# Two 384-byte tiles change pools and a 128-byte pad is added, so that most SBUF tiles begin at one address modulo 512

## The chip, the cores and the metric

The kernel runs on one core of a Trainium2 chip. The metric is the device time of one execution in microseconds. A core has a matrix engine (PE; its weight loads stand apart as PEld), a vector engine (DVE), a scalar engine (ACT), a general engine (POOL) and a queue engine (SP). All tiles that are named below lie in the on-chip memory SBUF, which has 128 partitions; an address is the byte at which a tile begins in each partition. PE writes its sums to PSUM, which the change does not touch.

## The reference, cut to what matters

One decoder layer on a sequence of 512 tokens of 1024 channels, in float32:

```python
mod = jax.nn.silu(c) @ w_ada[l] + b_ada[l]
sh1, sc1, g1, sh2, sc2, g2 = jnp.split(mod[:, None, :], 6, axis=-1)
h = modulate(rmsnorm(x, norm_mix_g[l]), sh1, sc1)
x = x + g1 * hybrid_mixer(h, ...)
h = modulate(rmsnorm(x, norm_ffn_g[l]), sh2, sc2)
x = x + g2 * swiglu(h, w_ffn_gate[l], w_ffn_up[l], w_ffn_down[l])
```

`hybrid_mixer` projects `h` to queries, keys, values and gates, runs two kinds of attention with 8 heads of 64 channels each, projects both results (`w_proj_a`, `w_proj_b`), mixes them with sigmoid gates and applies `w_out`. `swiglu` is `(silu(h @ w_gate) * (h @ w_up)) @ w_down` with 2816 inner channels. A last RMSNorm follows.

## The kernel before

Every product keeps float32 accuracy with three matmuls: an operand is split into a high part (`_hi`, or index 0) and the rest (`_lo`, or index 1), and PE adds high by high, high by low and low by high. A weight slab is loaded by a DMA into a tile `raw`; ACT copies its high part into a tile `hl`, DVE subtracts to get the low part. The `mm3` helper issues the three matmuls of one 128-channel step.

A matmul has two operands in SBUF. The stationary one, 128 columns, is loaded by PEld ahead of the matmul; the moving one, mostly 512 columns, streams through. They are, stage by stage, in the order of time (microseconds of the profiled execution):

- 0 to 75: first norm, transposes of `x` (tile `xt`), and the first projections; the values of the second attention have `h_hi`, `h_lo` stationary and `wvh` moving.
- 75 to 330: the other projections (stationary `hl`, moving `h_hi` or `h_lo`; outputs `mm`), interleaved with both attentions. Their matmuls have queries, keys, values and probabilities (`qa`, `qb`, `kb`, `ks`, `kw`, `vn`, `vball`, `ph`, `pl`, `E`) on both sides, and 128-column transposes with the constant `ident` moving.
- 343 to 417: eight blocks of the projected attention (`add_y`): stationary `hl`, moving `oah`, `oal`, `obh` (outputs `s`, `acc`), with gate projections (stationary `hl`, moving `h_hi`, `h_lo`, outputs `mm`) between them. 192 matmuls have `oah`, `oal` or `obh` moving.
- 417 to 465: `w_out` (`token_nodes`): stationary slices of `y`, moving `hl` or, for one of the four weight groups in the second half, `hlw`. 192 matmuls.
- 468 to 482: first feed-forward unit: stationary `hlk`, moving halves (256 columns) of `h_hi`, `h_lo`. 96 matmuls.
- 482 to 712: 21 feed-forward units (`ffn_unit`): stationary `hl`, moving `h_hi`, `h_lo`. 1008 matmuls.
- 712 to 835: down projection (`token_nodes`): stationary slices of `ah`, `al`, moving `hl`. 528 matmuls. The final norm follows.

The order on each engine comes from a list scheduler (`Sched`) that runs while the program is built, with its own table of costs; line 200, which the profile names for nearly every instruction, is its recording helper, so groups are told apart by tiles.

SBUF is handed out by tile pools. Pools lie one after the other in the order in which they are opened; a pool that is closed gives its room to those opened later. In order: `const`, `strm` (`raw`, `hl`), `hp` (`h_hi`, `h_lo`), `small`, `vx` (`vball`, `m0`, `x1t`), `att` (queries, keys, `vn`, `oah`, `oal`, `obh`, `hlk`, `hlw`), then `start`, later `ab` and `wk` or `yp` in its place (`ph`, `pl`, `E`, `y`). When `att` is closed, `fp` (`ah`, `al`, `sgt`, `gfb`, `o`) begins where `att` began. Tiles that share a tag take turns in the same buffers. Within a tile, the slices that PE reads begin at multiples of 512 bytes, except the 280-column weight rows (1120 bytes apart) and the 32-column slices of `kc`.

The two tiles that move are `gat` (the sigmoid gates of the first attention, written by ACT, read by DVE) and `sums` (row sums written by ACT, read by DVE). PE reads neither.

Of the kernel before, what the change touches and what calls it, by code (L numbers as in the profile page):

```python
# [6 lines left out]
F32 = mybir.dt.float32  # L7
# [7 lines left out]
NT = 4  # L15
# [273 lines left out]
def block_kernel(tc, x, c, w_ada, b_ada, norm_mix_g, w_in, cmp_pos_k, cmp_w1_k, cmp_w2_k,  # L289
# [19 lines left out]
    const = es.enter_context(tc.tile_pool(name="const", bufs=1))  # L309
    strm = es.enter_context(tc.tile_pool(name="strm", bufs=2))  # L310
    hp = es.enter_context(tc.tile_pool(name="hp", bufs=1))
    small = es.enter_context(tc.tile_pool(name="small", bufs=4))

    ident = const.tile([128, 128], F32, name="ident")
    make_identity(tc.nc, ident)
# [2 lines left out]

    vec = const.tile([128, 96], F32, name="vec")
    csil = const.tile([128, KT], F32, name="csil")  # L320
    VEC = {"gmix": 0, "bada": 8, "gffn": 56, "posk": 64, "posv": 80}

    def split_act(hi, lo, src):
# [64 lines left out]
    def fin_a(dst, sc, g, kk):  # L388
        nc.vector.scalar_tensor_tensor(dst[:, kk], sc[:, kk], 1.0, vec[:, VEC[g] + kk.start:VEC[g] + kk.stop],
                                       op0=OP.add, op1=OP.mult)  # L390

    def cols_of(ps, acc, dst, chunk, k0, n):
        for j in range(n):
            nc.tensor.matmul(ps[:, j:j + 1], acc[:, j * 128:(j + 1) * 128], ones[:, 0:1], start=True, stop=True)
        b = vec[:, VEC["bada"] + chunk * 8 + k0: VEC["bada"] + chunk * 8 + k0 + n]
        nc.vector.tensor_tensor(dst[:, k0:k0 + n], ps[:, 0:n], b, op=OP.add)
# [1 line left out]
    vx = es.enter_context(tc.tile_pool(name="vx", bufs=1))  # L398
    mid = ExitStack()
    att = mid.enter_context(tc.tile_pool(name="att", bufs=1))  # L400
    gat = att.tile([128, NT, 24], F32, name="gat")

    def qtile(name):
        return att.tile([128, S], R, name=name, tag="q2", bufs=10)
# [40 lines left out]

    kc = att.tile([128, 2, 64], R, name="kc")
    vcs = att.tile([64, 2, 2, 64], R, name="vcs")
    sums = att.tile([128, NT, 24], F32, name="sums")

    pss = ExitStack()  # L450
    pool = pss.enter_context(tc.tile_pool(name="psum", bufs=2, space=PS, reuse_waits="tile"))
# [11 lines left out]
    def stage_load(q, keys):  # L463
        for key, ap, n in (("gmix", norm_mix_g[0], 8), ("bada", b_ada[0], 48), ("gffn", norm_ffn_g[0], 8),
                           ("posk", cmp_pos_k[0].rearrange("j d -> (j d)"), 16),
                           ("posv", cmp_pos_v[0].rearrange("j d -> (j d)"), 16)):
            if key in keys:
                q.dma_start(stage[VEC[key]:VEC[key] + n] if VEC[key] < 56 else stage2[VEC[key] - 56:VEC[key] - 56 + n], rows(ap))

# [213 lines left out]
    def compress(which):  # L683
# [5 lines left out]
        def evac(last, fc, hmm):  # L689
# [13 lines left out]
            hi = lo = None  # L703
            pcol = vec[:, VEC[pos]:VEC[pos] + 16]
            for half in range(2):
# [111 lines left out]
    def add_ada(chunk, nh, dst, row, acc_tag, keys=(), rec=None):  # L817
# [19 lines left out]
        def post():  # L837
# [3 lines left out]
            else:  # L841
                o = VEC["bada"] + chunk * 8 + nh * 4
                nc.vector.tensor_tensor(dst[:, nh * 4:nh * 4 + 4], ps[:, 0:4], vec[:, o:o + 4], op=OP.add)
# [425 lines left out]
    def ada1_nodes(ci, n_cs, n_vec):  # L1269
# [37 lines left out]
        def fin():  # L1307
            for j in range(n):
                k = k0 + j
                g, b = VEC["gmix"] + k, VEC["bada"] + k  # L1310
                nc.scalar.activation(shcol[:, k:k + 1], cell["ps"][:, n + j:n + j + 1], AF.Identity, bias=vec[:, b:b + 1])
# [610 lines left out]
```

## Time and profile before

| | us |
|---|---|
| timed runs | 844.59, 842.13, 841.99; median 842.13 |
| span of the profiled execution, first to last instruction | 843.0 |
| PE busy | 810.5 |
| PEld busy | 664.7 |
| DVE busy | 512.9 |
| ACT busy | 390.2 |
| POOL busy | 37.5 |

The profile gives the profiled execution's span; no time outside the span is listed for it. Its 843.0 us lie inside the range of the three timed runs. A matmul's end is modelled in the profile and overlaps the next one's start, so a matmul's "duration" is longer than the distance to the next; distances are best read from the chain, where a piece gives the time of so many matmuls in a row.

### The profile page before, as it was taken

How to read it: one execution, taken by the hardware profiler on the slowest of the kernel's cores; microseconds unless marked ns; L12 is line 12 of the kernel's file. 1: busy time of each engine (PE TensorE's matmuls, PEld its weight loads, DVE VectorE, ACT ScalarE, POOL GpSimd, SP SyncE). 2: the span in 40 equal slices, each digit the busy share in tenths (PEclk: the TensorE clock that was granted, in tenths of full speed). 3: DMA queues.
4: the chain of work that ended last, by engine and by line, in shares of the span. 5: the costliest groups of instructions: out<-in, count | busy, mean ns of one | idle time of the engine just before them, and what ended most of it. 6: DMA issues, size and time to landing. Idle time of an engine off the chain costs nothing.

```text
span 843.0 us, 10574 instructions
## 1 busy us (share of the span) xinstructions
PE 810.5 (96%) x3881; PEld 664.7 (79%) x3881; DVE 512.9 (61%) x961; ACT 390.2 (46%) x737; POOL 37.5 (4%) x76
## 2 busy tenths in 40 slices
PE   5999998999999999999999899999999999999996
PEld 4777786788787887888888878888888888888884
DVE  3879988998789887755786653443333333225225
ACT  5566755566777887333444632232232223223123
POOL 3002203020000000000000000000000000000000
PEclk9999999999999999999999999999999999999998
DMA  9974233365311010773661463443333332232302
GB/s 285 314 205 125 76 82 119 101 156 138 88 51 50 1 51 26 225 222 114 214 219 31 126 195 114 140 128 99 100 101 100 100 95 89 92 100 84 110 7 100
DMA packets 130732, 100.56 MB, mean 119 GB/s; under 512 B 3804, under 2 KB 110404, under 8 KB 130680
## 3 DMA queue, kind: packets, MB, share of 16 engines
q1 hardware_dynamic: 129448, 96.59, 38.7%
q0 software_dynamic: 1136, 3.27, 1.6%
q8 instruction: 30, 0.49, 0.3%
q14 instruction: 22, 0.18, 0.1%
q10 hardware_dynamic: 96, 0.03, 0.0%
HBM read 95.12 MB, written 2.10 MB: 115 GB/s over the span
## 4 chain that ended last, share of the span: by engine, by line
PE 76%; DVE 10%; DMA 5%; ACT 5%; issue 2%; SPq 2%; POOL 1%; DVEq 0%; POOLq 0%; ACTq 0%
PE mm L200 31%; PE s L200 25%; PE acc L200 17%; PE tp L200 4%; DVE Rb L200 2%; SPq L200 2%; DVE hl L200 1%; DVE a L200 1%; DMA raw<-in_w_ada_dram 1%; DVE ada L200 1%; ACT hl L200 1%; DMA xt<-in_x_dram 1%; DMA wv<-in_w_in_dram 1%; DMA raw<-in_w_in_dram 1%; DMA kw<-kw 1%
## 5 line engine op out<-in xcount | busy, mean ns | idle before, releaser
L200 ACT ACTIVATE hl<-raw 128x1024 fp32r<-128x1024 f32 (+2 forms) x118 | 124.3, 1055 | 288.6 <-issue 142.1
L200 PE MATMUL mm<-h_hi,hl 128*128 128x512 f32 x736 | 249.4, 398 | 0.8 <-ACT s L200 0.8
L200 DVE TENSOR_TENSOR hl<-raw,hl 128x1024 fp32r<-128x1024 f32 (+2 forms) x118 | 143.3, 1215 | 151.5 <-ACT hl L200 151.1
L200 PEld LDWEIGHTS mm<-h_hi,hl 128*128 128x128 f32 x736 | 139.0, 189 | 28.9 <-ACT s L200 1.3
L200 PE MATMUL mm<-h_lo,hl 128*128 128x512 f32 x368 | 144.2, 392 | 0.2 <-DVE h_lo L200 0.2
L200 PEld LDWEIGHTS mm<-h_lo,hl 128*128 128x128 f32 x368 | 69.6, 189 | 12.9 <-DVE h_lo L200 0.6
L200 PE MATMUL s<-h_hi,hl 128*128 128x512 f32 x208 | 66.7, 391 | 0.0
L200 PE MATMUL acc<-h_hi,hl 128*128 128x512 f32 x208 | 66.1, 389 | 0.0
L200 PE MATMUL mm<-hl,ah 128*128 128x512 f32 x176 | 55.2, 395 | 0.0
L200 PE MATMUL s<-hl,ah 128*128 128x512 f32 x176 | 55.2, 395 | 0.0
L200 ACT ACTIVATE ph<-tp 128x512 fp32r<-128x512 f32 (+1 forms) x72 | 36.1, 524 | 21.1 <-PE tp L200 16.0
L200 PEld LDWEIGHTS s<-h_hi,hl 128*128 128x128 f32 x208 | 39.0, 188 | 8.3 <-issue 0.2
L200 DVE TENSOR_TENSOR pl<-tp,ph 128x512 fp32r<-128x512 f32 (+1 forms) x72 | 40.9, 597 | 7.6 <-ACT ph L200 7.3
L200 PEld LDWEIGHTS acc<-h_hi,hl 128*128 128x128 f32 x208 | 39.1, 188 | 8.1
L200 PE MATMUL s<-h_lo,hl 128*128 128x512 f32 x104 | 40.5, 389 | 0.0
L200 PE MATMUL acc<-h_lo,hl 128*128 128x512 f32 x104 | 40.5, 389 | 0.0
L200 ACT ACTIVATE E<-T,m 128x256 f32<-128x256 f32 (+3 forms) x64 | 35.4, 554 | 9.3 <-DVE m L200 8.8
L200 PEld LDWEIGHTS s<-hl,ah 128*128 128x128 f32 x176 | 33.2, 188 | 7.7
L200 PEld LDWEIGHTS mm<-hl,ah 128*128 128x128 f32 x176 | 33.1, 188 | 7.7
L200 PE MATMUL mm<-hl,al 128*128 128x512 f32 x88 | 34.7, 395 | 0.0
L200 PE MATMUL s<-hl,al 128*128 128x512 f32 x88 | 34.7, 395 | 0.0
L200 DVE SCALAR_TENSOR_TENSOR adaacc<-raw,csil,adaacc 128x512 f32<-128x512 f32 x42 | 31.0, 746 | 5.8 <-DMA raw<-in_w_ada_dram 5.4
(281 smaller groups left out, 1326.5 us busy)
## 6 DMA issues: line engine op xcount, KB each, us to landing
raw<-in_w_in_dram SPq DMA_DIRECT2D x32, 512.0 KB, 4.7
raw<-in_w_ada_dram SPq DMA_DIRECT2D x32, 512.0 KB, 4.1
raw<-in_w_ffn_gate_dram SPq DMA_DIRECT2D x22, 512.0 KB, 3.9
raw<-in_w_ffn_up_dram SPq DMA_DIRECT2D x22, 512.0 KB, 5.0
raw<-in_w_ffn_down_dram SPq DMA_DIRECT2D x22, 512.0 KB, 3.9
adaraw<-in_w_ada_dram SPq DMA_DIRECT2D x32, 256.0 KB, 5.4
raw<-in_w_out_dram SPq DMA_DIRECT2D x8, 512.0 KB, 4.7
xt<-in_x_dram SPq DMA_DIRECT2D x4, 512.0 KB, 6.5
```

What stands on the lines that cost most here:

```text
L200: return f(*args, **kw)
```

## The change

`gat` and `sums`, 384 bytes per partition each, are taken from the pool `const` and no longer from `att`; an unused tile of 128 bytes is opened first in the pool `small`. So `strm` and `hp` begin 768 bytes later, `vx` and what follows 896 bytes later, and what follows the two tiles in `att` 512 or 128 bytes later than before.

```diff
     small = es.enter_context(tc.tile_pool(name="small", bufs=4))
+    small.tile([128, 32], F32, name="pad", tag="pad", bufs=1)
...
     csil = const.tile([128, KT], F32, name="csil")
+    gat = const.tile([128, NT, 24], F32, name="gat")
+    sums = const.tile([128, NT, 24], F32, name="sums")
...
     att = mid.enter_context(tc.tile_pool(name="att", bufs=1))
-    gat = att.tile([128, NT, 24], F32, name="gat")
...
     vcs = att.tile([64, 2, 2, 64], R, name="vcs")
-    sums = att.tile([128, NT, 24], F32, name="sums")
```

The addresses modulo 512 at which tiles begin in the two built programs:

| tiles | pool | before | after |
|---|---|---|---|
| `raw`, `hl` | strm | 320 | 64 |
| `h_hi`, `h_lo` | hp | 320 | 64 |
| `vball`, `m0`, `x1t` | vx | 192 | 64 |
| `kc`, `vcs` | att | 64 | 64 |
| queries, keys, `vn`, `wvh`, `oah`, `oal`, `obh`, `hlk`, `hlw` | att | 448 | 64 |
| `xt` | start | 448 | 64 |
| `ph`, `pl`, `E`, `a`, `y` | wk, yp | 448 | 64 |
| `ah`, `al`, `sgt`, `gfb`, `o` | fp | 192 | 64 |
| `ident`, `ones` | const | 128 | 128 |
| `csil` | const | 0 | 0 |
| `adaraw` | start | 96 | 224 |

So four kinds of tile that PE reads are not at 64 afterwards: `ident`, `ones`, `csil` and `adaraw`. They serve the transposes and the small conditioning products.

On every engine the two programs have the same instructions in the same order. One wait differs: POOL's DMA that loads `gfb` waits for one more DMA queue.

## Rows read from the trace of the kernel before

**Rows 1.** The page: span, busy time by engine, granted clock in 40 slices

```profile
span 843.0 us, 10574 instructions
...
PE 810.5 (96%) x3881; PEld 664.7 (79%) x3881; DVE 512.9 (61%) x961; ACT 390.2 (46%) x737; POOL 37.5 (4%) x76
...
PEclk9999999999999999999999999999999999999998
```

**Rows 2.** Stretches: length, busy time (instructions) of PE, PEld, DVE, ACT, POOL; clock; DMA

```profile
343.20:416.90 73.70, 73.70 (x323) 59.85 (x323) 47.86 (x62) 27.56 (x37) 0.00 (x0) 1.00 0.64 195
...
482.00:701.00 219.00, 218.85 (x963) 180.26 (x962) 86.19 (x99) 63.99 (x83) 0.00 (x0) 1.00 0.40 115
712.00:834.90 122.90, 122.89 (x529) 99.28 (x527) 42.81 (x62) 29.64 (x41) 0.00 (x0) 1.00 0.24 78
```

**Rows 3.** The chain, last feed-forward units and down projection: start, us, what, matmuls

```profile
592.50 10.88 PE mm L200 x48
...
712.19 2.79 PE mm L200 x12
...
834.91 0.02 issue
```

**Rows 4.** The chain through `add_y` and `w_out`, same columns

```profile
343.19 2.79 PE s L200 x12
...
354.38 5.45 PE mm L200 x24
...
416.90 1.40 PE mm L200 x6
...
439.19 1.64 PE tp L200 x10
440.84 11.26 PE s L200 x48
...
452.97 5.57 PE acc L200 x24
```

**Rows 5.** Matmuls that read `hl`, 600 to 700 us: duration ns min/median/max, starts

```profile
L200 PE MATMUL s<-h_hi,hl x96: 389/389/389, 608.7 to 690.0; 128*128 128x512 f32 x96
```

**Rows 6.** The same view of `hl`, 343.2 to 354.3 us

```profile
L200 PE MATMUL acc<-obh,hl x24: 392/395/398, 345.8 to 354.0; 128*128 128x512 f32 x24
```

**Rows 7.** The same view of `hl`, 354.6 to 359.6 us

```profile
L200 PE MATMUL mm<-h_hi,hl x16: 389/389/393, 354.2 to 359.4; 128*128 128x512 f32 x16
```

**Rows 8.** The same view of `hlw`, 447.0 to 447.5 us

```profile
L200 PE MATMUL s<-hlw,y x3: 389/389/393, 446.8 to 447.3; 128*128 128x512 f32 x3
```

**Rows 9.** The same view of `hl`, 448.4 to 451.2 us

```profile
L200 PE MATMUL s<-hl,y x13: 392/398/398, 448.2 to 451.0; 128*128 128x512 f32 x13
```

**Rows 10.** The same view of `hl`, 720 to 830 us

```profile
L200 PE MATMUL s<-hl,ah x168: 390/393/404, 720.4 to 825.9; 128*128 128x512 f32 x168
```

**Rows 11.** The same view of `hlk`, 474 to 481.4 us; the chain there

```profile
L200 PE MATMUL s<-h_hi,hlk x17: 278/281/285, 473.9 to 481.2; 128*128 128x256 f32 x17
...
478.69 2.86 PE s L200 x24
```

**Rows 12.** The chain, 240 to 330 us: shares by line; one piece

```profile
by line: PE mm L200 37.3%; PE acc L200 23.4%; PE s L200 21.2%; PE tp L200 17.2%; ACT half L200 0.7%; ACT oah L200 0.6%; issue 0.0%
...
244.27 2.08 PE mm L200 x9
```

**Rows 13.** The chain, 75 to 240 us, then 0 to 75 us: shares by line

```profile
by line: PE mm L200 29.6%; DVE Rb L200 10.3%; PE tp L200 6.9%; DVE a L200 6.8%; PE acc L200 6.1%; issue 4.4%; DVE hl L200 4.2%; PE s L200 4.1%; DMA kw<-kw 3.5%; DVE pl L200 3.4%; POOL a L200 3.3%; DVE qa L200 2.5%; ACT hl L200 2.3%; DVE kb 
...
by line: SPq L200 17.0%; DVE ada L200 9.7%; DMA xt<-in_x_dram 8.7%; DMA wv<-in_w_in_dram 8.2%; DMA raw<-in_w_in_dram 7.9%; PE mm L200 7.5%; DMA adaraw<-in_w_ada_dram 7.2%; issue 4.8%; ACT hl L200 4.2%; DVE kb L200 3.7%; PE tp L200 3.5%; ACT
```

**Rows 14.** Instructions that write or read `gfb`: duration ns, starts

```profile
L200 DVE TENSOR_TENSOR x1t<-x1t,gfb x4: 679/682/691, 763.3 to 777.2; 128x512 f32<-128x512 f32 x4
...
L200 POOL DMA_DIRECT2D gfb<-in_norm_final_g_dram x1: 542/542/542, 466.3 to 466.3; - x1
...
DMA to landing us min/median/max: 6.1/6.1/6.1
```

## The prediction

> **What bounds the kernel now.** I read the page first. PE is busy for 810.5 of 843.0 us and the granted clock is at or near full speed in every slice, its level of 2.4 GHz [rows 1]. PE being busy does not yet mean that it sets the end, so I read the stretches and the chain next. Between 343 and 417, 482 and 701, 712 and 834.9 us PE has next to no idle time, DVE is busy for 65%, 39% and 35% of the stretch and ACT for 37%, 29% and 24%, all at a clock of 1.00 [rows 2]. The chain there is matmul after matmul [rows 3, 4]. From 240 to 330 us PE also holds 99.1% of the chain [rows 12]. From 75 to 240 us its lines hold 46.7%, and before 75 us about 11% [rows 13]. So from about 240 us on, time that a matmul saves is time off the end; earlier, less than half of it is.
>
> Then I asked what a matmul costs. The instruction is the same in both halves of the feed-forward network, 128 by 128 stationary and 512 columns moving. The last 528 matmuls of the up projections run from 592.50 to 712.19 us, 119.69 us or 226.7 ns each (48 of them take 10.88 us). The 528 of the down projection run from 712.19 to 834.91 us, 122.72 us or 232.4 ns each [rows 3]. Clock and instruction are equal, and nothing waits. The durations show the same in another form: 389 ns for every one in the first stage, 390 to 404 ns in the second [rows 5, 10]. They differ by the 6 ns of the distances.
>
> What differs? In the up projections both operands begin at 320 modulo 512. In the down projection the stationary one begins at 192 and the moving one at 320. Two more places separate the address from other causes. In `add_y` the stationary `hl` (320) meets `obh` (448): 392 to 398 ns. The gate projections in the same stretch, with the same stationary tile, the same roles and the same neighbours at work, but moving `h_hi` (320), have 389 to 393 [rows 6, 7]. By the chain, 48 matmuls of the first sort take 11.19 us (343.19 to 354.38), 24 of the second 5.45 [rows 4]. And in `w_out` the stationary `y` (448) meets `hlw` (448) in six matmuls: the last three have a median of 389 ns. It meets `hl` (320) right behind: a median of 398 [rows 8, 9]. This has the roles of the down projection. So equal addresses give 389 in either role, and unequal ones more.
>
> PEld is busy for 180 of 219 us while PE is busy for all of it [rows 2], so a matmul's weights are loaded while the one before streams. I read this as two streams of reads that collide now and then; with equal starts they settle into a rhythm where they don't. The trace shows the rhythm, not its cause.
>
> **A rule that speaks against it.** The Trainium skill, page "SBUF — State Buffer", section "Who interferes with whom", says that PE has two independent read ports, one for moving data and one for weights, and never waits on anyone. By it the address could not matter, and the time would stay at 842.1. The spacings above (226.7 and 232.4 ns) speak against it.
>
> **The change part by part.** The diff removes and adds no instruction, and the order on each engine is the same. What changes is where tiles begin: nearly all at 64.
>
> *Down projection.* 528 matmuls from 192 against 320 to 64 against 64: 122.72 to 119.69 us, **3.03 us**.
>
> *`add_y`.* 192 matmuls; 48 take 11.19 us against 10.88, four such stretches 1.24 us. Conditioning products interrupt it in two places, after which the spacing must settle again: **1.15 us**, at least 1.0.
>
> *`w_out`.* The first 96 take 22.29 us (416.90 to 439.19); of the second 96, 72 take 11.26 + 5.57 = 16.83 us [rows 4], so all of them 22.44. Against 21.76 at 96 times 226.7 ns that is 0.53 + 0.68 = 1.21 us. The 24 with `hlw` begin in step already and transposes and small products cut in four times: **1.05 us**, at least 0.9.
>
> *First feed-forward unit.* 96 matmuls of 256 columns; 24 take 2.86 us, 119 ns each, with durations from 278 to 285 [rows 11]. No row shows 256 columns with equal addresses. Half of 226.7 would be 113.3 ns, so the gain lies between nothing and 0.56 us: **0.25**, since the shorter matmul may have no rhythm of its own.
>
> *Attention, 240 to 330 us.* Here the matmuls have equal addresses within a pair (448 with 448, 320 with 320) but change between the two every few instructions, and transposes with `ident` (128) stand between. Nine take 2.08 us, 231 ns each [rows 12]. The chain's three lines of matmuls hold 81.9% of 90 us, 73.7 us; all of it at 226.7 instead of 231.1 would give 1.40 us. The change of addresses between pairs goes, the transposes stay, since `ident` stays at 128. Settling takes about three matmuls [rows 8] and a run between transposes has some ten. I take a third: **0.45**, from nothing to 1.40.
>
> *75 to 240 us.* The same three lines hold 39.8% of 165 us, 65.7 us; the same 1.9% of it is 1.25 us. When PE gets ahead here, DVE's scans and conversions [rows 13] are late next, so **0.3**, from nothing to 1.25. Before 75 us the 96 matmuls with `wvh` could give 0.5 us, but DMA and DVE hold that chain: **0.05**.
>
> *Costs.* The pad costs no instruction. `gat` and `sums` are written and read as before. POOL's load of `gfb` waits for one more DMA queue; it was issued at 466.3 us, took 6.1 us, and is first read at 763.3 [rows 14], so 290 us cover it, nothing but the program's end is queued behind it on POOL, and without cover the price would be about the 6.1 us. Should PE overtake the conversions of the down projection, `hl` would be late next; DVE is busy for 35% there and ACT for 24% [rows 2], and 2.5% more speed does not reach them.
>
> **Sum.** 3.03 + 1.15 + 1.05 + 0.25 + 0.45 + 0.3 + 0.05 = 6.3 us. From the profiled span of 843.0 us that leaves 836.7. The span is 0.9 us above the median of the timed runs, 842.13; taken from the median the forecast is **835.8 us**. By the lower bounds the gain is 3.0 + 1.0 + 0.9 = 4.9 us (837.2), by the upper ones 3.03 + 1.24 + 1.21 + 0.56 + 1.40 + 1.25 + 0.5 = 9.2 us (833.0).
>
> **The rivals.** *The address is not it.* The spacing might follow from which tile is read and how it was written. Then every stage keeps its spacing: 842.1 us. For it: I have no experiment, only stages that differ in more than one thing and none with the address alone changed. Against it: two places where role, load and clock are equal [rows 6 to 9]. Chance 0.09. By the Trainium skill's rule cited above this is the case to be expected.
>
> *Only the feature-major role settles.* If slices of 128 columns out of a long tile (`y`, `ah`) upset the rhythm as stationary operand over a longer run, the down projection and `w_out` keep their 232 ns, and 6.3 less 4.1 remains, 2.2 us: 839.9. For it: the evidence for that role is three matmuls [rows 8]. Against it: they do settle, at once. Chance 0.07.
>
> *Slower: one address for everybody.* With nearly all tiles at 64, ACT and DVE, which write `ah`, `al` and `sgt` at 192 during the feed-forward units, now start in step with PE's reads. If that breaks the rhythm of the 1008 matmuls there and keeps it from forming elsewhere, they cost 5.7 ns more each, 5.7 us: 847.9. It decides for slower, beyond what can be measured, once some 440 of them are lost and nothing is won (2.5 us by 5.7 ns). Against it: `raw` and `hl`, which ACT and DVE read and write in the same units, begin at 320 as PE's operands do, and every matmul there shows 389 [rows 5]. Chance 0.05.
>
> **How the numbers follow.** The forecast has 0.79 and its own range 833.0 to 837.2. A range up to 840.0 takes in the second rival and leaves out the first and the third, 0.14, and a little at the edges. A measurement here can tell about 0.3%, 2.5 us, from no change, so faster means below 839.6: the forecast's 0.79. Same holds the first rival and the second, 0.16; slower the third, 0.05.
>
> **What would show it.** Right, step by step: pieces of 12 in the down projection at 2.72 instead of 2.79 us and durations of 389 throughout; 48 matmuls of `add_y` in 10.9 us; `w_out` at 21.9 us per 96; the up projections unchanged at 5.44 per 24; transposes unchanged; durations of `mm` before 330 us a little nearer to 389. Wrong: a down projection that still takes 122 to 123 us (first or second rival, told apart by `add_y`), up projections above 5.44 per 24 (third), or matmuls that are faster while a new wait of PE for `hl` or for DVE's results appears in the chain.

## The result, and the profile after

The changed kernel takes 839.06 us against 843.93 us of the kernel before (medians of six executions each, 836.89 to 840.41 and 841.99 to 845.90): a ratio of 0.9940, 95% interval 0.9925 to 0.9954. It is faster, by 4.9 us. The profiled execution took 839.45 us; its span is 837.7 us, 5.3 us shorter than that of [rows 1], so some 1.75 us of an execution lie outside the span.

The page of the changed kernel, span and busy time by engine:

```profile
span 837.7 us, 10574 instructions
...
PE 804.7 (96%) x3881; PEld 663.6 (79%) x3881; DVE 512.9 (61%) x961; ACT 390.4 (47%) x737; POOL 37.5 (4%) x76
```

PE has lost 5.8 us of busy time with the same 3881 instructions; the other engines have what they had, and the mean granted clock of both executions is 0.995. The stretch that answers to the last one of [rows 2], with the same columns:

```profile
709.90:829.60 119.70, 119.70 (x529) 98.78 (x527) 42.77 (x62) 29.65 (x41) 0.00 (x0) 1.00 0.25 80
```

The down projection now takes 119.70 us, at a clock of 1.00 as before, with PE busy throughout. No new wait has come in there. The chain of the changed kernel, in order of time (start, us, what, instructions), answers to [rows 3, 4, 11, 12]:

```profile
140.30 4.08 PE mm L200 x12
...
243.92 2.08 PE mm L200 x9
...
336.91 5.78 PE mm L200 x24
342.69 2.72 PE s L200 x12
...
415.26 1.36 PE mm L200 x6
...
420.70 4.08 PE mm L200 x18
...
450.59 5.49 PE acc L200 x24
...
476.12 2.89 PE s L200 x24
...
492.65 4.43 DMA raw<-in_w_ada_dram
...
502.31 5.44 PE acc L200 x24
...
709.93 2.72 PE mm L200 x12
```

Three rows of the chain of the kernel before that were not shown there, for the same places:

```profile
140.04 4.15 PE mm L200 x12
...
337.41 5.78 PE mm L200 x24
...
495.33 4.01 DMA raw<-in_w_ada_dram
```

Starts at the same place of the two chains give a ledger of the time saved so far: −0.26 us at 140, 0.35 at 244, 0.50 at 337 (337.41 less 336.91), 1.64 at the start of `w_out` (416.90 less 415.26), 2.38 at its last 48 matmuls (452.97 less 450.59), 2.57 inside the first feed-forward unit (478.69 less 476.12), 2.68 at the start of the DMA wait (495.33 less 492.65), 2.26 at the start of the down projection (712.19 less 709.93), 5.3 at the end. So the down projection gave 3.0, `add_y` 1.14, `w_out` and its tail about 0.95, all before that 0.50; a landing that took 4.43 instead of 4.01 us took back 0.4.

Matmuls by tile in the changed kernel (duration ns min/median/max, starts) answer to [rows 5, 6, 9, 10, 11]:

```profile
L200 PE MATMUL acc<-obh,hl x24: 389/389/389, 345.2 to 353.2; 128*128 128x512 f32 x24
...
L200 PE MATMUL s<-hl,y x48: 388/389/389, 416.5 to 436.6; 128*128 128x512 f32 x48
...
L200 PE MATMUL s<-h_hi,hlk x22: 279/283/364, 469.9 to 478.7; 128*128 128x256 f32 x22
...
L200 PE MATMUL s<-h_hi,hl x96: 389/389/389, 606.4 to 687.8; 128*128 128x512 f32 x96
...
L200 PE MATMUL s<-hl,ah x168: 389/389/389, 717.9 to 820.8; 128*128 128x512 f32 x168
```

`obh`, `y` and `ah`, which had 392 to 404 ns, are at 389 like the up projections. Only the matmuls of 256 columns with `hlk` have gained nothing: their median is 283 ns, 281 before.

### The profile page after: what moved, and what is told of

Same layout as the page of the kernel before. It is cut to its first block, busy times and chain, and to the rows that moved or that the text cites. A ratio compares the mean times of both kernels' runs of the same rounds, so it can differ in the third digit from the quotient of the medians.

```text
span 837.7 us, 10574 instructions
## 1 busy us (share of the span) xinstructions
PE 804.7 (96%) x3881; PEld 663.6 (79%) x3881; DVE 512.9 (61%) x961; ACT 390.4 (47%) x737; POOL 37.5 (4%) x76
## 4 chain that ended last, share of the span: by engine, by line
PE 74%; DVE 11%; ACT 6%; DMA 4%; issue 2%; SPq 1%; POOL 1%; DVEq 0%; ACTq 0%; POOLq 0%
PE mm L200 29%; PE s L200 24%; PE acc L200 17%; PE tp L200 5%; DVE Rb L200 2%; DMA adaraw<-in_w_ada_dram 2%; DVE hl L200 1%; DVE a L200 1%; ACT hl L200 1%; DMA raw<-in_w_ada_dram 1%; ACT hf L200 1%; DVE ada L200 1%; SPq L200 1%; DVE pl L200 1%; DMA kw<-kw 1%
## 5 line engine op out<-in xcount | busy, mean ns | idle before, releaser
L200 DVE CUSTOM_DVE_ANT_0 T<-s,Dm 128x256 f32<-128x256 f32 (+3 forms) x64 | 29.5, 485 | 7.9 <-PE s L200 6.6
```

The source lines that it names most:

```text
L200: return f(*args, **kw)
```

## The experiments

All ten have the same instructions in the same order on every engine. Besides start addresses only what POOL's load of `gfb` waits for differs (in two kernels with one more wait instruction), and in the pad alone not even that: its waits are those of the kernel before. Below, "distance" is the difference modulo 512 of the starts of a matmul's two operands, and a spacing is a piece of the chain divided by its matmuls. The first four kernels ran beside one another, compared with the kernel before at 844.09 us.

### The pad alone

```diff
+    small.tile([128, 32], F32, name="pad", tag="pad", bufs=1)
```

Added to the kernel before; `gat` and `sums` stay in `att`. The weights' tiles, `h_hi`, `h_lo`, `ah` and `al` begin at 320, `oah`, `oal`, `obh`, `y` and `hlk` at 64.

> The kernel before with the pad alone; gat and sums stay in att. The weights (raw, hl) and h stay at 320 modulo 512, the attention tiles, y and the add_y operands go to 64, and ah, al go to 320, as hl. Same instructions in the same order. Theory A (a matmul's spacing depends on whether its two operands begin at the same address modulo 512): the down projection settles, pieces of 12 at 2.72 us, 119.7 us for 528; add_y stays near 11.2 us for 48 and w_out near 22.3 us for 96, since 64 meets 320 there; span about 840.0, 3.0 us under that of before. Theory B (what counts is the absolute address, 64 being a good one): the down projection stays at 2.79 us for 12, add_y and w_out may gain; span 841 to 843. Theory C (address does not count, something else in the change helped): span between 837.7 and 843.0 without a difference by stage.

Measured: 837.37 us, ratio 0.9932 (0.9918 to 0.9946). The chain of this kernel:

```profile
343.60 2.72 PE acc L200 x12
...
422.97 4.08 PE s L200 x18
...
710.33 2.72 PE s L200 x12
```

The down projection settles, as expected. But `add_y` and `w_out` settle too, 226.7 ns each, although 64 meets 320 there. So equality modulo 512 is not needed; modulo 256 the two starts are equal. The theory on which the prediction stood was too narrow, and the two moved tiles were not needed.

### The move alone

```diff
-    small.tile([128, 32], F32, name="pad", tag="pad", bufs=1)
```

Taken out of the changed kernel. The weights' tiles, `h_hi` and `h_lo` begin at 64, all that follows at 448: distance 384, which is 128 modulo 256.

> The changed kernel without the pad: gat and sums in const. The weights and h are at 64 modulo 512, all of attention, y, the add_y operands, ah and al at 448. Theory A: down projection, add_y and w_out all stay unequal and keep 2.79 us for 12, 11.2 for 48, 22.3 for 96; attention as before; span 842.5 to 843.5. Theory B: whatever has hl or h at 64 gains, so the up projections can't be told, but add_y (stationary hl at 64) would gain some; span 841 or less. Theory C: the move of the two tiles is what helped, span near 837.7.

Measured: 844.78 us, ratio 1.0007 (0.9991 to 1.0024). The chain:

```profile
346.02 2.80 PE acc L200 x12
...
422.51 4.19 PE mm L200 x18
...
712.21 2.79 PE mm L200 x12
```

Every stage is as before, 233, 233 and 232.5 ns. The whole gain comes with the pad.

### Everything at 160

```diff
+    const.tile([128, 24], F32, name="pad2")
```

Added to the changed kernel, so that the common start is 160 instead of 64.

> The changed kernel with 96 more bytes in const, ahead of everything: all that was at 64 modulo 512 is at 160; ident and ones stay at 128. Theory A: nothing changes against the changed kernel: down projection 2.72 us for 12, add_y 10.9 for 48, w_out 21.9 for 96, span 837.4 to 838.0. Theory B: with 64 left, the stages go back to 2.79, 11.2 and 22.3, span about 843.

Measured: 837.90 us, ratio 0.9931 (0.9920 to 0.9943). The chain, at three places:

```profile
140.08 2.75 PE mm L200 x12
...
347.38 2.72 PE s L200 x12
...
712.06 2.72 PE s L200 x12
```

The common start itself doesn't matter: the settled spacing is 226.7 ns at 64 and at 160, as it was at 320 in the up projections before. (The first row is taken up below.)

### `ident` and `ones` at 64 as well

`vec`, `csil` and `acol` are handed out ahead of them.

```diff
+    vec = const.tile([128, 96], F32, name="vec")
+    csil = const.tile([128, KT], F32, name="csil")
+    acol = const.tile([128, KT], F32, name="acol")
...
     ident = const.tile([128, 128], F32, name="ident")
```

> The changed kernel with ident and ones also at 64 modulo 512 (they are handed out behind vec, csil and acol; no byte more). Theory A extended to the transposes: between 75 and 337 us the matmuls no longer lose their rhythm at each transpose, since ident meets E, a and xn at the same address; the changed kernel saved only some 0.5 us there, this one saves another 0.3 to 1.0 us, span 836.7 to 837.4. Rival: the rhythm is lost at a transpose because of its 128 columns and its waits, not its address: span 837.4 to 838.0, and the transposes keep their 109 ns either way.

Measured: 838.37 us, ratio 0.9942 (0.9923 to 0.9962). The chain in the attention, the piece of nine matmuls of [rows 12]:

```profile
243.38 2.08 PE mm L200 x9
...
336.38 5.73 PE mm L200 x24
```

Nine still take 2.08 us, with `ident` at 128 or at 64, and from there to the piece at the end of the attention it is 93.00 us, 92.99 in the changed kernel (243.92 to 336.91). What keeps the attention from settling is not the address of the transposes.

It isn't unsettled throughout. In the changed kernel the next run, of twelve matmuls from 248.5 us on, settles within three; there the matmuls by tile, 249.1 to 251.2 us, are

```profile
L200 PE MATMUL mm<-h_hi,hl x7: 389/389/389, 249.0 to 251.1; 128*128 128x512 f32 x7
```

and the same seven were at 393 to 397 ns in the kernel before. So after a break the spacing takes more matmuls to settle at one place than at another, and the run of nine is over before it has.

### Distances of 32, 64, 96, 192 and 256

Three kernels, each the changed one with pads ahead of `kc` in `att`, of `y` in `yp` and of `ah` in `fp`; the middle one is shown, and the others have 8, 8, 24 and 24, 40, 16 columns. One profiled execution each.

```diff
+    att.tile([128, 16], F32, name="pada")
...
+    yp.tile([128, 32], F32, name="pady", tag="pady", bufs=1)
...
+    fp.tile([128, 8], F32, name="padf", tag="padf", bufs=1)
```

> The changed kernel with three unused tiles, so that three stages get other distances between their two operands: add_y 32 bytes, w_out 64 (hlw against y 32), down projection 96. Hlk also moves to 96. Theory A2 (equal modulo 256 settles, anything else does not, as the pad-alone run with its distance of 256 in add_y and w_out suggests): all three go back to 11.2 us for 48, 22.3 for 96 and 2.79 for 12, span about 843. Theory D (only the half-way distance of 128 collides): they stay at 10.9, 21.9 and 2.72, span about 837.7. In between: small distances stay settled and larger ones do not.

> As the run before, with distances of 64 bytes in add_y, 192 in w_out (128 against hlw) and 32 in the down projection. Theory A2: 11.2 for 48, 22.3 for 96, 2.79 for 12, span about 843. Theory D: 10.9, 21.9 and 2.72, span about 837.7. In between: 32 settles in the down projection and 192 behaves as 64 does.

> As the run before, with distances of 96 bytes in add_y, 256 in w_out and 64 in the down projection. Theory A (modulo 512): all three unsettled, 11.2, 22.3 and 2.79. Theory A2 (modulo 256): w_out settles at 21.9 for 96, the other two do not. Theory D: all three settle.

Measured: 843.71, 844.72 and 844.78 us, beside 843.32 us of the kernel before. The chains of the three in `add_y`, `w_out` and the down projection (of the second also in the first feed-forward unit, from 477.65):

```profile
343.19 2.80 PE acc L200 x12
...
424.09 4.20 PE s L200 x18
...
712.94 2.81 PE s L200 x12
```

```profile
345.89 2.75 PE acc L200 x12
...
417.68 1.37 PE s L200 x6
...
425.94 4.15 PE s L200 x18
...
477.65 2.72 PE s L200 x24
...
714.47 2.80 PE s L200 x12
```

```profile
345.47 2.80 PE acc L200 x12
...
418.01 1.36 PE s L200 x6
...
426.19 4.12 PE s L200 x18
...
714.51 2.80 PE s L200 x12
```

A distance of 32 costs as much as 128 did (2.80 per 12 in `add_y` and in the down projection), and 96 as much or a little more (2.80 and 2.81). So it isn't the distance of 128 alone that collides, as a rival had it. A distance of 64 is half settled in `add_y` (2.75, 229 ns) and not at all in the down projection (2.80) or `w_out` (4.20).

`w_out` at 256 in the third kernel is better than unequal starts but not at 4.08, for a reason that the expectations had overlooked. The last of the eight `y` tiles, `y7`, is taken from `att` and not from `yp`, so there it begins at 160, 96 bytes from `hl`, while the other seven are at 320. The first 24 matmuls don't read `y7`, and from the seventh on they are at 226.7 ns (1.36 per 6). The pieces of 18 that follow end with three that do, and take 4.12. So `w_out` does settle at 256, and the last experiment tries 256 again. In the second kernel too `y7` stands apart, at 128 and the others at 256: without it 6 matmuls take 1.37 us, 228.3 ns each, with it 18 take 4.15.

With the sign of the distance the values at 64 and 192 agree. In `add_y` of the second kernel the moving operand begins 64 bytes above the stationary one; in `w_out` of that kernel it begins 192 below, which modulo 256 is 64 above again. Both are half settled, 229.2 and 228.3 ns. In the two places at 233.3, `w_out` of the first kernel and the down projection of the third, it begins 64 below. This was read from the rows afterwards and no run was made for it.

Nor are equal starts the best for 256 columns. With `hlk` at 128 and `h_hi`, `h_lo` at 64, in the second kernel, 24 matmuls of the first feed-forward unit take 2.72 us, 113.3 ns each; with equal starts they take 2.89, and before, with `hlk` at 448 and the others at 320, 2.86.

### `h_hi` and `h_lo` apart from the weights

```diff
-    small.tile([128, 32], F32, name="pad", tag="pad", bufs=1)
...
+    hp.tile([128, 32], F32, name="pad", tag="pad", bufs=1)
```

The pad of the changed kernel stands ahead of `h_hi` and `h_lo`, which then begin at 192; all else is at 64. This spoils a stage that had been settled from the start.

> The changed kernel with its pad in front of h_hi and h_lo in place of behind them: h at 192 modulo 512, all else as changed (64). Theory A2: the 1008 matmuls of 512 columns in the up projections lose their rhythm, 5.58 us for 24 in place of 5.44, 5.7 us in all, and so do the projections before; down projection, add_y and w_out stay settled at 2.72, 10.9 and 21.9 (the gate projections between the add_y blocks go from 5.45 to 5.6 for 24); span 843.5 to 845. Rival (only long slices as stationary operand, as in down projection and w_out, need equal addresses): up projections stay at 5.44, span about 837.7.

Measured: 846.83 us, ratio 1.0037 (1.0022 to 1.0051), so slower than the kernel before, where the changed kernel has 0.9940. The chain:

```profile
346.48 2.72 PE s L200 x12
...
351.92 5.59 PE mm L200 x24
...
591.40 11.15 PE mm L200 x48
...
716.86 2.72 PE s L200 x12
```

The up projections, which had 10.88 us per 48 in both kernels, take 11.15, and 5.6 ns by 1008 matmuls is 5.6 us. `add_y` and the down projection in the same execution keep 2.72. The gate projections lose the same way (5.59 per 24, 5.44 in the changed kernel); what the projections before 417 us add was not taken apart. The profiled execution is the fastest of the twelve, and its span, 841.9 us, lies under the 843.5 to 845 that were expected; 1.3 us of that is the granted clock at 140 us, which the last section takes up (2.79 us for twelve matmuls, 4.08 in the changed kernel). The start address sets the spacing in both roles and in both directions.

### `al` apart from `ah`

```diff
+    fp.tile([128, 32], F32, name="padl", tag="padl", bufs=1)
```

In the changed kernel, between `ah` (64) and `al` (now 192). One of three matmuls of the down projection reads `al`.

> The changed kernel with a 128-byte pad between ah and al, so that ah, h_hi, h_lo and the weights' tiles all stay at 64 modulo 512 and al alone moves to 192. In the down projection two matmuls of three read ah or the weights' high part with ah, one reads al. Theory A2 as a matter of each single matmul (a matmul is late only when its own weight load and the stream beside it differ modulo 256): of the three matmuls of a chunk only those next to al are late, so the mean excess lies between a third and two thirds of the 6 to 7 ns of the other distances: 12 matmuls take about 2.74 to 2.77 us and the stage gives back 1.0 to 2.0 of its 3.0 us. Rival theory P (the rhythm is a state that one unequal matmul breaks for its neighbours too): 2.79 to 2.80 per 12, all of the 3.0 us lost. Rival theory H (only the operand read most often counts): 2.72 to 2.73 as in the changed kernel. All other stages as in the changed kernel: 2.72 per 12 in add_y, 5.44 per 24 in the up projections.

Measured: 843.49 us in one execution, beside 842.58 of the kernel before. A piece of the chain, the matmuls of this kernel by tile, 715 to 828 us, and three matmuls that follow one another (the same view for 730.20 to 730.25 and 730.7 to 730.8 us):

```profile
719.94 2.77 PE s L200 x12
...
L200 PE MATMUL s<-hl,ah x174: 389/392/396, 714.9 to 824.7; 128*128 128x512 f32 x174
...
L200 PE MATMUL s<-hl,al x88: 397/397/397, 714.7 to 824.9; 128*128 128x512 f32 x88
...
L200 PE MATMUL mm<-hl,ah x1: 389/389/389, 730.2 to 730.2; 128*128 128x512 f32 x1
...
L200 PE MATMUL mm<-hl,ah x1: 396/396/396, 730.4 to 730.4; 128*128 128x512 f32 x1
L200 PE MATMUL mm<-hl,al x1: 397/397/397, 730.6 to 730.6; 128*128 128x512 f32 x1
```

Every matmul with `al` is late, at 397 ns. Those with `ah`, whose own two starts are equal, have a median of 392 only because they are of two kinds: the one right behind an `al` is on time, at 389, and the one right ahead of an `al` is late, at 396. The load of `al`'s weights begins 3 ns after the latter, so it runs beside that matmul's stream. From start to start the three take 226.7, 232.6 and 234.1 ns on average over the stage. Twelve take 2.77 us (231 ns): the upper edge of what was expected if a matmul is late only next to an unequal load, and short of the 2.79 to 2.80 of a rhythm that is lost altogether. Some three quarters of the stage's loss come with one unequal matmul in three, since the one ahead of it is late too. The total of this execution says little about the stage: at the DMA wait, well ahead of it, it was already 1.55 us behind the changed kernel (494.20 and 492.65).

### 160 and 256 once more

```diff
+    yp.tile([128, 40], F32, name="pady", tag="pady", bufs=1)
...
+    fp.tile([128, 64], F32, name="padf", tag="padf", bufs=1)
```

Added to the changed kernel: `y` at 224 against 64, `ah` and `al` at 320 against 64.

> The changed kernel with a 160-byte pad ahead of y and a 256-byte pad ahead of ah and al: in w_out y begins at 224 and hl and hlw at 64 (distance 160), in the down projection ah and al begin at 320 and hl at 64 (distance 256); add_y and the up projections as in the changed kernel, 2.72 per 12 and 5.44 per 24. Theory A2 (the starts must be equal modulo 256): the down projection keeps 2.72 us per 12 matmuls and its 119.7 us; w_out loses its rhythm, 4.15 to 4.21 per 18 as against 4.08 in the changed kernel, and most of its 1.0 us. Theory A (modulo 512): the down projection goes back to 2.78 to 2.80 per 12 and some 122.7 us, w_out as in A2. Rival R (the closer distances only shift the phase, and 160 happens to do well as 64 did in add_y): w_out at 4.08 to 4.13.

Measured: 838.43 us in one execution, beside 843.82. The chain:

```profile
423.06 4.20 PE s L200 x18
...
711.60 2.72 PE s L200 x12
```

The down projection keeps its 226.7 ns over all 528 matmuls at a distance of 256, while `w_out` at 160 has 233. So of the distances tried equality modulo 256 settles long runs of 512 columns, and the rival that other distances might do as well falls for 160.

All spacings together, in ns for one 512-column matmul:

| distance | modulo 256 | spacing |
|---|---|---|
| 0 | 0 | 226.7 in `add_y`, `w_out`, the up projections and the down projection of the changed kernel |
| 256 | 0 | 226.7 (`add_y`, `w_out` with the pad alone; down projection at 256; `w_out` of the third kernel of distances without `y7`); 228.9 (the same with `y7` at 96) |
| 32 | 32 | 233.3 (`add_y`, down projection) |
| 64 | 64 | 229.2 (`add_y`, moving above stationary); 233.3 (`w_out`, down projection, moving below) |
| 96 | 96 | 233.3 (`add_y`); 234.2 (down projection) |
| 128 or 384 | 128 | 231.7 to 233.3 (before; the move alone; `h` apart) |
| 160 | 160 | 233.3 (`w_out`) |
| 192 | 192 | 228.3 (`w_out` without `y7`, moving below); 230.6 (the same with `y7` at 64) |

## Why the prediction was right

**The mechanism.** "Equal addresses give 389 in either role, and unequal ones more" held in both directions: the change brings `add_y`, `w_out` and the down projection to it, and moving `h_hi` away takes the up projections out of it. The rival that address is not it falls, above all with the pad alone, which differs from the kernel before in nothing but addresses. That rival had the Trainium skill, page "SBUF — State Buffer", section "Who interferes with whom", on its side, which says that PE's two read ports are independent and that PE never waits; as the prediction read this, no start address could have changed a spacing, and the runs show up to 7.5 ns. Why they do is not shown: the trace has no view of SBUF's ports.

**The modulus.** The prediction took equality modulo 512 as the condition. The pad alone and the run at 160 and 256 show that 256 is enough. This changed no number of the forecast, since the changed kernel has equality modulo 512 anyway, but it hid that one line of the change does all of it.

**The terms.** Down projection: forecast 3.03, measured 3.0 (119.70 us, as foretold). `add_y`: 1.15, measured 1.14. `w_out`: 1.05, measured about 0.95. These three make 5.1 of the 5.3 us.

Three small terms were mis-sized. The first feed-forward unit was to give 0.25 us and gave nothing: its 24 matmuls take 2.89 us, 2.86 before, so matmuls of 256 columns stay at 119 to 120 ns with equal starts. The prediction's reason, that they may have no rhythm of their own, is not it: at another distance they come to 113.3 ns, which is half of 226.7 and would have given the 0.56 us of its upper bound. Attention was to give 0.45 between 240 and 330 us; between the pieces at 244 and 337 it gave 0.15. The nine matmuls of [rows 12] still take 2.08 us. The prediction thought that switching between two addresses broke the rhythm there; with one address for all of them, and with `ident` there too, it is still broken. Short runs, with transposes and waits between them, are what remains as the reason; the run of twelve that settles fits it, but it was not tried. From 75 to 240 us 0.3 was forecast; 0.35 stands in the ledger at 244, made of 0.26 lost up to 140 us and 0.61 gained after it. How much of either is the scatter of a single execution can't be told from it.

**What was overlooked.** "From about 240 us on, time that a matmul saves is time off the end" doesn't hold at 485 to 502 us, where the chain passes through two DMAs and DVE. The second DMA took 0.42 us longer and the saving fell from 2.68 to 2.26. In the six kernels of the experiments whose chain passes there it took 4.18 to 4.55 us, whether the spacings had settled or not, so it is not the price of the change; the 4.01 before was the short one.

**The total.** 5.3 us of span instead of 6.3: 0.25, 0.3 and 0.42 of those three points account for it. The forecast of 835.8 also started from a median of three executions, 842.13, which happened to be low; with three more it is 843.93, and 6.3 less than that is 837.6, against the measured 839.06. Comparing that median with the span of 843.0 hid it, since some 1.75 us of an execution lie outside the span. The forecast's own range, 833.0 to 837.2, did not hold 839.06; the range up to 840.0 did, and it had been widened for the second rival, which did not come about. That the time fell inside is in part luck. The saving of 4.9 us is the sum of the lower bounds.

**The second rival**, that only the feature-major role settles, falls too: with `y` and `ah` stationary, `w_out` takes 4.08 per 18 and the down projection 2.72 per 12. Its 839.9 us is nearer to 839.06 than the forecast is; the stages tell them apart, the total does not.

**The slower rival**, one address for everybody, falls: the up projections keep 5.44 us per 24 while ACT and DVE write `ah`, `al` and `sgt` from the same start. POOL's longer wait for `gfb` appears nowhere in the chain.

**The best version** is the pad alone, 0.9932 against 0.9940 of the whole change. The intervals overlap, so they are equal as far as was measured; it needs one line.

## What to carry to other kernels

Where PE runs matmul after matmul and two stages with the same shape differ in spacing by 2 or 3%, compare the start addresses of stationary and moving operand before looking for a wait: here, among multiples of 32 bytes, they had to agree modulo 256, and one unused tile of 128 bytes was worth 0.7%. It counts only where PE sets the end and long runs of 512 columns have nothing between them; here three such stages with 912 matmuls gave nearly all of it, and the attention next to nothing. Matmuls of 256 columns gained nothing from equal starts. And since any tile that is added or resized shifts all that is opened after it, an edit that has nothing to do with PE can lose such a rhythm: the same pad, one pool earlier, cost 0.4%.

## What was not expected of the hardware

That 256 bytes apart is as good as equal (226.7 ns both), and 32 as bad as 128 (233 ns). That 64 is half good with the moving operand above the stationary one (229.2 and, at 192 below, 228.3 ns) and bad with it below (233.3 ns). That 256 columns settle at 113.3 ns with the moving operand 64 below, where 512 columns don't, and stay at 120 with equal starts. That one unequal matmul in three costs three quarters of the loss, because the one ahead of it is late as well.

The granted clock makes part of the scatter. At 140 us PE goes on after the chain has waited 4.34 us for POOL's `a`. The twelve matmuls there take 4.15 us in the kernel before, 4.08 in the changed one and 2.75 with everything at 160, as the first rows of the three chains above show. The stretch from 138 to 146 us (length, busy time of the engines, granted clock, DMA), in the changed kernel and then with everything at 160:

```profile
138.00:146.00 8.00, 6.17 (x23) 5.07 (x24) 4.73 (x9) 3.39 (x9) 2.12 (x3) 0.79 0.42 131
```

```profile
138.00:146.00 8.00, 6.24 (x32) 5.27 (x33) 6.21 (x12) 3.87 (x10) 2.87 (x4) 1.00 0.46 131
```

A mean of 0.79 is part of the stretch at the level of 1.2 GHz; 1.00 is 2.4 GHz throughout. The wait ahead of it is the same in all three. Of the twelve profiled executions seven have the slower stretch (4.08 to 4.34 us for the twelve matmuls) and five the faster one (2.75 to 2.79), with settled and unsettled spacings among both. It gives or takes 1.3 to 1.4 us of an execution, and two single spans compared without it would have put that down to the edit.
